# Seven block products in place of eight in the feed-forward networks of a two-block transformer kernel

## The chip, the cores and the metric

The kernel runs on one core of one Trainium2 chip. The metric is the device time of one execution in microseconds (us). Engines are named as in the profile: PE (TensorE, matmuls; PEld is its weight load), DVE (VectorE), ACT (ScalarE), POOL (GpSimd), SP (SyncE, which here issues the loads).

## What is computed

256 rows of 1024 float32 values pass through a first block (attention and mLSTM mixers, then a feed-forward network) and twice through a second block (network, mixer with attention over a memory, network). That makes five feed-forward networks, all of one size, 1024 to 2 x 2816 and back:

```
def swiglu(h, w_gate, w_up, w_down):
    return (jax.nn.silu(h @ w_gate) * (h @ w_up)) @ w_down

def second_block(...):
    for i in range(DEPTH_2):
        h = rmsnorm(x, ffn1_norm[i])
        x = x + 0.5 * swiglu(h, ffn1_w_gate[i], ffn1_w_up[i], ffn1_w_down[i])
        ...
        x = x + jnp.concatenate([o_s, o_m], axis=-1) @ w_out[i]
        h = rmsnorm(x, ffn2_norm[i])
        x = x + 0.5 * swiglu(h, ffn2_w_gate[i], ffn2_w_up[i], ffn2_w_down[i])
    return x
```

## The kernel before

**Tiles.** The rows are two tiles of 128, t = 0 and 1. The activations stand transposed in SBUF: u[t] is 8 tiles of 128 (of K = 1024) by 128 rows. The weights lie in DRAM as 228 pieces of 128 x 2048 float32 (1 MB): a piece is 512 of K by 512 columns (gate-up), or 256 of K by 1024 columns (down). SP loads them in the order of use into RAW_BUFS = 3 slots (`load_to`, L199).

**A float32 product in three matmuls.** Each operand is split into a high part, rounded to fp32r by a copy on ACT, and the rest, by a subtraction on DVE (`split`, L204 and L205: `wh`, `wl` for weights, `uh`/`ul` and `hh`/`hl` for activations). `mm3` then issues three matmuls of 512 columns: high by high, low by high, high by low. A piece is split in two halves of 128 x 1024, each in two parts of 512 columns (SPLIT_W); W_BUFS = 8 such halves of `wh` and of `wl` stand in SBUF, and `split_to` runs SPLIT_AHEAD = 4 halves ahead of the matmuls. A half's slot is free again when both row tiles have used it.

**A feed-forward network** (`ffn_body`) goes over NJ = 11 blocks of 256 hidden columns. For block j and tile t, `gu(t, j)` forms a bank of 256 gate and 256 up columns (8 x 3 = 24 matmuls); the gate is x(1 + tanh(x/2))/2 by a Tanh on ACT (L355), DVE's L356, and DVE's L358, which multiplies in the up half and gives `hid`. `turn` flips `hid` with the identity on PE (L154, four flips of 128 x 128 for both tiles) and splits it into `hh` and `hl`. `dn(t, j)` multiplies it into two banks that stay open over the whole network (12 matmuls). The order on PE is written out by hand: gu(0, j), dn(0, j-1), gu(1, j), dn(1, j-1), 72 matmuls and 4 flips a round; `fin(t)` (L402) adds the result to the residual. All the other engines' orders are the scheduler's, with elementwise work marked as urgent by `crit`.

**Between networks** stand the mixers: projections by the same `lin`, attention, norms (`row_rstd`, with POOL's powers at L261), and the projection `w_out` (L1197 adds it to the residual h).

## Time and profile before

| | |
|---|---|
| time, median of 3 runs | 1405.89 us (1405.14 to 1406.78) |
| time of the profiled execution | 1406.4 us, of which its span 1404.6 us |
| PE busy | 1385.3 us, 99% of the span, 6598 matmuls |
| DVE busy | 922.8 us, 66% |
| ACT busy | 763.6 us, 54% |
| POOL busy | 58.2 us, 4% |
| weight loads | 243.09 MB in SP's queue |

The profiled execution is 0.5 us above the median. A share of busy time is a mean over the networks, where all rounds are alike, and the mixers, where engines wait for one another; the stretches are read one by one below.

### The profile page before, as it was taken

To read this page: it belongs to the slowest core of one execution; us is meant where nothing else is said; L and a number is where in the kernel's file an instruction comes from. 1 tells how busy PE (TensorE), PEld (TensorE's weight loads), DVE (VectorE), ACT (ScalarE), POOL (GpSimd) and SP (SyncE) were. 2 spreads that over 40 slices of the span, in tenths; PEclk is the share of its full clock that TensorE was granted. 3 is DMA by queue.
4 is the path that set the end of the run, shared out by engine and by line. 5 is a ranking of instruction groups with operands and counts; after the bars stand their busy time and mean duration, and the time that the engine had idled before them with its cause. 6 is when DMAs were issued, how large, how long until landed. Compare 5 with 4: busy or idle time off the path is not lost.

```text
span 1404.6 us, 18011 instructions
## 1 busy us (share of the span) xinstructions
PE 1385.3 (99%) x6598; PEld 1126.6 (80%) x6598; DVE 922.8 (66%) x1789; ACT 763.6 (54%) x1527; POOL 58.2 (4%) x59
## 2 busy tenths in 40 slices
PE   8999999999999999999999999999999989999998
PEld 6777888888888888877888888888888767888887
DVE  7866587555585575768576665765756787755554
ACT  6556555444474454668565444644545568544442
POOL 0000000000010000022000000000000121000000
PEclk9999999999999999999999999999999999999999
DMA  8534546555446455454255555555454532455540
GB/s 291 174 122 158 180 142 237 192 191 189 180 157 233 180 180 180 168 197 161 91 183 191 195 187 194 207 191 197 164 206 155 182 120 94 172 188 194 192 180 30
DMA packets 37081, 246.59 MB, mean 176 GB/s; under 512 B 4736, under 2 KB 5760, under 8 KB 8064
## 3 DMA queue, kind: packets, MB, share of 16 engines
q1 hardware_dynamic: 35568, 243.09, 48.2%
q10 hardware_dynamic: 1424, 2.34, 0.5%
q8 instruction: 52, 0.85, 0.2%
q14 instruction: 37, 0.30, 0.1%
HBM read 244.37 MB, written 1.05 MB: 175 GB/s over the span
## 4 chain that ended last, share of the span: by engine, by line
PE 90%; DVE 6%; POOL 2%; ACT 1%; issue 1%; DMA 0%; SPq 0%; DVEq 0%; POOLq 0%; ACTq 0%
PE bank L149 86%; PE trbank L154 4%; POOL fac L261 2%; DVE wl L205 2%; DVE ms L953 1%; ACT p L454 1%; DVE nm L452 1%; DVE z L957 1%; DMA h<-in_x_dram 0%; DVE p L464 0%; DVE p L450 0%; DVE z L1015 0%; DVE p L1052 0%; DVE z L1017 0%; DVE z L1018 0%
## 5 line engine op out<-in xcount | busy, mean ns | idle before, releaser
L205 DVE TENSOR_TENSOR wl<-raw,wh 128x512 fp32r<-128x512 f32 x908 | 580.5, 686 | 194.4 <-ACT wh L204 187.6
L204 ACT CAST wh<-raw 128x512 fp32r<-128x512 f32 x908 | 513.0, 619 | 238.2 <-PE bank L149 227.9
L149 PE MATMUL bank<-wh,uh 128*128 128x512 f32 x1248 | 501.3, 402 | 0.0
L149 PE MATMUL bank<-wl,uh 128*128 128x512 f32 x1248 | 489.5, 392 | 0.0
L149 PE MATMUL bank<-wh,ul 128*128 128x512 f32 x1248 | 489.3, 392 | 0.0
L149 PEld LDWEIGHTS bank<-wh,ul 128*128 128x128 f32 x1248 | 234.6, 188 | 52.6
L149 PEld LDWEIGHTS bank<-wh,uh 128*128 128x128 f32 x1248 | 234.9, 188 | 48.8 <-issue 1.9
L149 PEld LDWEIGHTS bank<-wl,uh 128*128 128x128 f32 x1248 | 235.2, 188 | 46.1 <-DVE wl L205 0.3
L149 PE MATMUL bank<-wh,hh 128*128 128x512 f32 x440 | 172.8, 393 | 0.0
L149 PE MATMUL bank<-wl,hh 128*128 128x512 f32 x440 | 172.0, 391 | 0.0
L149 PE MATMUL bank<-wh,hl 128*128 128x512 f32 x440 | 172.0, 391 | 0.0
L355 ACT ACTIVATE th<-bank,rs 128x256 f32<-128x256 f32 x110 | 52.3, 475 | 179.2 <-PE bank L149 178.4
L356 DVE SCALAR_TENSOR_TENSOR th<-th,bank 128x256 f32<-128x256 f32 x110 | 46.3, 421 | 153.2 <-ACT th L355 153.2
L149 PEld LDWEIGHTS bank<-wl,hh 128*128 128x128 f32 x440 | 82.7, 188 | 18.0
L149 PEld LDWEIGHTS bank<-wh,hl 128*128 128x128 f32 x440 | 82.6, 188 | 17.9
L149 PEld LDWEIGHTS bank<-wh,hh 128*128 128x128 f32 x440 | 82.7, 188 | 17.6
L204 ACT CAST hh<-trbank 128x512 fp32r<-128x512 f32 (+1 forms) x60 | 33.1, 551 | 55.8 <-PE trbank L154 55.8
L261 POOL TENSOR_TENSOR r<-ms,mhalf 128x1 f32<-128x1 f32 x22 | 18.4, 838 | 909.5 <-DVE ms L271 909.5
L358 DVE SCALAR_TENSOR_TENSOR hid<-bank,rs,th 128x256 f32<-128x256 f32 x110 | 53.2, 484 | 3.6
L205 DVE TENSOR_TENSOR hl<-trbank,hh 128x512 fp32r<-128x512 f32 (+1 forms) x60 | 38.8, 646 | 16.5 <-ACT hh L204 13.5
L261 POOL TENSOR_TENSOR fac<-ms,mhalf 128x4 f32<-128x4 f32 (+2 forms) x26 | 38.4, 1477 | 246.8 <-DVE ms L954 139.3
L154 PEld LDWEIGHTS trbank<-cst,hid 128*128 128x128 f32 x220 | 27.6, 140 | 8.1
(223 smaller groups left out, 940.1 us busy)
## 6 DMA issues: line engine op xcount, KB each, us to landing
raw<-in_weights_dram SPq DMA_DIRECT2D x226, 1024.0 KB, 4.9
mem<-in_mem_dram ACTq DMA_DIRECT2D x4, 512.0 KB, 5.5
Tb<-in_rel_dram SPq DMA_DIRECT2D x3, 512.0 KB, 5.8
h<-in_x_dram SPq DMA_DIRECT2D x4, 256.0 KB, 3.8
raw<-in_weights_dram SPq DMA_DIRECT2D x2, 512.0 KB, 7.4
gf<-in_rows_dram SPq DMA_DIRECT2D x1, 512.0 KB, 4.1
out_dram<-h SPq DMA_DIRECT2D x2, 256.0 KB, 2.0
out_dram<-h SPq DMA_DIRECT2D x4, 128.0 KB, 1.8
```

The lines of the kernel that those rows point to most:

```text
L149: pe.matmul(out=out, lhsT=lhsT, rhs=rhs, start=start, stop=stop)
L154: pe.transpose(out=out, in_=in_, identity=ident if identity is None else identity)
L204: act.copy(out=hi, in_=src)
L205: dve.tensor_tensor(out=lo, in0=src, in1=hi.bitcast(F32), op=ALU.subtract)
L261: pool.tensor_tensor(out=dst, in0=src, in1=mhalf[:, 0:n], op=ALU.pow)
L355: act.activation(out=th, in_=acc[:, 0:256], func=AF.Tanh, scale=rh[t])
L356: dve.scalar_tensor_tensor(out=th, in0=th, scalar=1.0, in1=acc[:, 0:256], op0=ALU.add, op1=ALU.mult)
L358: dve.scalar_tensor_tensor(out=hd, in0=acc[:, 256:512], scalar=r2[t], in1=th, op0=ALU.mult, op1=ALU.mult)
L452: dve.tensor_reduce(out=nm, in_=s, axis=AX.X, op=ALU.max, negate=True)
L454: act.activation(out=p[:, j, a, 0:n], in_=s[:, j], func=AF.Exp, bias=nm[:, j:j + 1], accum_out=sums[:, j, a:a + 1])
L953: dve.tensor_reduce(out=ms, in_=sq, axis=AX.X, op=ALU.add)
L957: dve.tensor_tensor(out=v, in0=v, in1=fac.unsqueeze(2).to_broadcast([128, n, w]), op=ALU.mult)
```

## The change

In each network the first 5 blocks stay as they were (order gu(0), gu(1), dn(0), dn(1)). The other six form GROUPS = 3 groups of two blocks. The gate-up product of two blocks is a 2 x 2 by 2 x 2 block product: the row tiles and the halves of K on one side, the halves of K and the two blocks on the other. It is formed from seven block products P1 to P7 instead of eight (Strassen's scheme in Winograd's form), each 12 matmuls. For this

- four sums of activation blocks are formed and split once a network (`group_operands`, after the first block);
- four sums of weight pieces are formed in each group: two by DVE (L267, `raw<-raw,rawx` and `tn<-raw,rawx`, 128 x 1024 twice each), two by accumulating DMAs that POOL issues (L277: `rawx<-rawx`, for P7, and `tn<-raw`, for P4). `rawx` are two slots for the pieces b12 and b22, `tn` is one slot for a sum;
- the bank results are joined by seven DVE adds of 128 x 512 (L562, `jo`) and a copy on ACT (L576, c11).

The gate is one Silu on ACT; L356 of before has no counterpart. Splits are 1024 wide (SPLIT_W), ACT's copies of weights keep their written order (`in_order`), W_BUFS is 6, and `w_out` goes over columns first. The memory tile has one buffer for two. The load order of a group is b11, dn_a, b12, b22, b21, dn_b. ACT loads its tables 8 times for 3.

```diff
+P_FFN = 3 * NJ
 
 RAW_BUFS = 3
-W_BUFS = 8
+W_BUFS = 6
 C_BUFS = 11
 C2_BUFS = 10
 SPLIT_AHEAD = 4
 LOAD_AHEAD = 2
 CRIT = 300
-SPLIT_W = 512
+SPLIT_W = 1024
+
+GROUPS = 3
...
     def load_to(n):
         while stream["load"] < min(n, NP):
             i = stream["load"]
-            r = wp.tile([128, 2048], F32, tag="raw", bufs=RAW_BUFS, name="raw")
+            if i in kept:
+                r = kept[i][0].tile([128, 2048], F32, tag="tx", bufs=2, name="rawx")
+            else:
+                r = wp.tile([128, 2048], F32, tag="raw", bufs=RAW_BUFS, name="raw")
             n_dma = 2 if i == 0 else 1
             for q in range(n_dma):
                 w = 2048 // n_dma
-                nc.sync.dma_start(out=r[:, w * q:w * q + w], in_=weights[i, :, w * q:w * q + w])
+                nc.sync.dma_start(out=r[:, w * q:w * q + w], in_=weights[piece_at.get(i, i), :, w * q:w * q + w])
             raws[i] = r
             stream["load"] += 1
...
     def split(hi, lo, src):
-        act.copy(out=hi, in_=src)
+        c = act.copy(out=hi, in_=src)
         dve.tensor_tensor(out=lo, in0=src, in1=hi.bitcast(F32), op=ALU.subtract)
+        return c
+
+    order = [None]
+
+    def in_order(inst):
+
+        if order[0] is not None:
+            tc.add_manual_dep(inst.ins, order[0].ins.name,
+                              mybir.DependencyInfo(mybir.DependencyClass.NoSync, mybir.DependencyReason.DATA),
+                              reason="order of the operands")
+        order[0] = inst
 
     def split_to(n):
 
-        while stream["split"] < min(n, 2 * NP):
-            i, m = divmod(stream["split"], 2)
-            load_to(i + 1 + LOAD_AHEAD)
-            r = raws[i]
+        while stream["split"] < min(n, len(jobs)):
+            key, piece, work = jobs[stream["split"]]
+            load_to(piece + 1 + LOAD_AHEAD)
+            r = work()
             hi = wp.tile([128, 1024], FR, tag="wh", bufs=W_BUFS, name="wh")
             lo = wp.tile([128, 1024], FR, tag="wl", bufs=W_BUFS, name="wl")
             for s in range(0, 1024, SPLIT_W):
-                split(hi[:, s:s + SPLIT_W], lo[:, s:s + SPLIT_W], r[:, 1024 * m + s:1024 * m + s + SPLIT_W])
-            parts[i, m] = (hi, lo)
+                in_order(split(hi[:, s:s + SPLIT_W], lo[:, s:s + SPLIT_W], r[:, s:s + SPLIT_W]))
+            parts[key] = (hi, lo)
             stream["split"] += 1
...
+    def group_jobs(i, pool_, dn):
+
+
+        b11, b12, b22, b21 = i, i + 2, i + 3, i + 4
+        kept[b12] = kept[b22] = pool_
+        s = lambda m: slice(1024 * m, 1024 * m + 1024)
+        total = []
+
+        def job(name, piece, work):
+            for m in range(2):
+                add_job(((i, name), m), piece, lambda m=m: work(m))
+
+        def add(out, a, b):
+            dve.tensor_tensor(out=out, in0=a, in1=b, op=ALU.add)
+
+        def t2(m):
+            if m == 0:
+                total.append(pool_[0].tile([128, 2048], F32, tag="tn", bufs=1, name="tn"))
+            add(raws[b11][:, s(m)], raws[b11][:, s(m)], raws[b12][:, s(m)])
+            add(total[0][:, s(m)], raws[b11][:, s(m)], raws[b22][:, s(m)])
+            return total[0][:, s(m)]
+
+        def dma_add(out, a):
+            pool.dma_start(out=out, in_=a, accum_op=ALU.add)
+
+        def b21_(m):
+            if m == 0:
+                dma_add(raws[b12], raws[b22])
+            return raws[b21][:, s(m)]
+
+        def b11_(m):
+            if m == 0:
+                dma_add(total[0], raws[b21])
+            return raws[b11][:, s(m)]
+
+        def t3(m):
+            return raws[b12][:, s(m)]
+
+        def t4(m):
+            return total[0][:, s(m)]
+
+        job("P1", b11, lambda m: raws[b11][:, s(m)])
+        plain(dn[0])
+        job("P6", b22, t2)
+        job("P2", b21, b21_)
+        job("P5", b21, b11_)
+        plain(dn[1])
+        job("P3", b21, lambda m: raws[b22][:, s(m)])
+        job("P7", b21, t3)
+        job("P4", b21, t4)
...
+        nc_ = NJ - 2 * GROUPS
...
+        for j in range(nc_):
+            take(("gu", j), 2)
+            if 1 <= j < nc_ - 1:
+                take(("dn", j - 1))
...
+        for g in range(GROUPS):
+            j = nc_ + 2 * g
+            a, b = (j - 2, j - 1) if g == 0 else (j - 1, j - 2)
+            plan["group", g] = i
+            plan["dn", a], plan["dn", b] = i + 1, i + 5
+            g0, g1 = source(("gu", j)), source(("gu", j + 1))
+            piece_at.update(enumerate((g0, source(("dn", a)), g1, g1 + 1, g0 + 1, source(("dn", b))), i))
+            group_jobs(i, plan["pool"], (i + 1, i + 5))
+            i += 6
+        for j in ((NJ - 2, NJ - 1) if GROUPS else ()):
...
-            acc = lin(u[t], gup(j))
-            ev = Ready()
-            if j == 0:
-                with crit():
-                    rh[t], r2[t] = scaled(r[t], 0.5), scaled(r[t], r[t], 0.5)
-
+        hidT, hid_ready, hids = {}, {}, {}
+        n_conv = NJ - 2 * GROUPS
+
+        def element(t, j, acc):
+
+            hid_ready[t, j] = Ready()
             with crit():
                 th = fp.tile([128, 256], F32, tag="th", name="th")
-                act.activation(out=th, in_=acc[:, 0:256], func=AF.Tanh, scale=rh[t])
-                dve.scalar_tensor_tensor(out=th, in0=th, scalar=1.0, in1=acc[:, 0:256], op0=ALU.add, op1=ALU.mult)
-                hd = fp.tile([128, 256], F32, tag="hid", bufs=4, name="hid")
-                dve.scalar_tensor_tensor(out=hd, in0=acc[:, 256:512], scalar=r2[t], in1=th, op0=ALU.mult, op1=ALU.mult)
-            hids[t] = hd
-            hid_ready[t, j] = ev
-            if j == NJ - 1:
-                side.spawn(turn((t,), j))
-            elif t == 1:
-                side.spawn(turn((0, 1), j))
+                act.activation(out=th, in_=acc[:, 0:256], func=AF.Silu, scale=r[t])
+                hd = fp.tile([128, 256], F32, tag="hid", bufs=5, name="hid")
+                dve.scalar_tensor_tensor(out=hd, in0=acc[:, 256:512], scalar=r[t], in1=th, op0=ALU.mult, op1=ALU.mult)
+            hids[t, j] = hd
+
+        def gu(t, j):
+            i = plan["gu", j]
+            acc = lin(u[t], (i, i + 1))
+            element(t, j, acc)
+            if t == 1:
+                side.spawn(turn((0, 1), j, 3.46))
             side.run()
...
+            hh = fp.tile([128, 2 * n, 128], FR, tag=f"hh{n}{ts[0]}", bufs=n, name="hh")
+            hl = fp.tile([128, 2 * n, 128], FR, tag=f"hl{n}{ts[0]}", bufs=n, name="hl")
...
+        def group_operands():
+            x11, x12, x21, x22 = (full.pop((id(u[t][2]), k)) for t in range(2) for k in (0, 4))
+            sh = fp.tile([128, 4, 4, 128], FR, tag="sh", bufs=1, name="sh")
+            sl = fp.tile([128, 4, 4, 128], FR, tag="sl", bufs=1, name="sl")
+
+            dve.tensor_tensor(out=x22, in0=x21, in1=x22, op=ALU.subtract)
+            dve.tensor_tensor(out=x21, in0=x11, in1=x21, op=ALU.subtract)
+            dve.tensor_tensor(out=x11, in0=x22, in1=x11, op=ALU.subtract)
+            dve.tensor_tensor(out=x12, in0=x12, in1=x11, op=ALU.add)
+            for n, (name, x) in enumerate((("P6", x11), ("P5", x22), ("P7", x21), ("P3", x12))):
+                split(sh[:, n], sl[:, n], x)
+                S[name] = sh[:, n], sl[:, n]
+            for name, t, k in (("P1", 0, 0), ("P2", 0, 4), ("P4", 1, 4)):
+                S[name] = u[t][0][:, k:k + 4], u[t][1][:, k:k + 4]
+
+        def group(g):
+
+            j = n_conv + 2 * g
+            a, b = (j - 2, j - 1) if g == 0 else (j - 1, j - 2)
+            last = g == GROUPS - 1
+            i = plan["group", g]
+
+            def joined(x, y, op, into=None):
+                o = fp.tile([128, 512], F32, tag="jo", bufs=4, name="jo") if into is None else into
+                with crit():
+                    dve.tensor_tensor(out=o, in0=x, in1=y, op=op)
+                return o
+
+            def prod(name):
+                acc = bank()
+                xh, xl = S[name]
+                for k in range(4):
+                    wh, wl = half((i, name), k // 2, 512)
+                    mm3(acc, xh[:, k], xl[:, k], wh[:, k % 2], wl[:, k % 2], k == 0, k == 3)
+                return acc
+
+            c11 = fp.tile([128, 512], F32, tag="jo", bufs=4, name="jo")
+            p1_ = prod("P1")
+            with crit():
+                act.copy(out=c11, in_=p1_)
+            dn(1, a)
+            dn(0, a)
+            U = joined(prod("P6"), c11, ALU.add)
+            joined(prod("P2"), c11, ALU.add, c11)
+            element(0, j, c11)
+            if last:
+                side.spawn(turn((0,), j, 4.2))
+            V = joined(prod("P5"), U, ALU.subtract)
+            dn(0, b)
+            c12 = joined(prod("P3"), V, ALU.add)
+            element(0, j + 1, c12)
+            if last:
+                side.spawn(turn((0,), j + 1, 4.2))
+            dn(1, b)
+            p7 = prod("P7")
+            joined(V, p7, ALU.subtract, V)
+            element(1, j + 1, V)
+            joined(p7, U, ALU.add, U)
+            side.spawn(turn((1,) if last else (0, 1), j + 1, 4.9))
+            joined(prod("P4"), U, ALU.add, U)
+            element(1, j, U)
+            side.spawn(turn((1,) if last else (0, 1), j, 4.2))
...
+        for j in range(n_conv):
+            more = 1 <= j < n_conv - 1
             gu(0, j)
-            if j:
+            gu(1, j)
+            if more:
                 dn(0, j - 1)
-            gu(1, j)
-            if j:
                 dn(1, j - 1)
-            if during and j == 5:
+            if j == 0:
+                group_operands()
+            if during and j == n_conv - 1:
                 during()
-        j = NJ - 1
-        gu(0, j)
-        dn(0, j - 1)
-        gu(1, j)
-        dn(1, j - 1, (0,))
+        for g in range(GROUPS):
+            group(g)
+        j = NJ - 2
         dn(0, j)
+        dn(1, j + 1, (0,))
+        dn(0, j + 1, by_c=True)
         fin(0)
-        dn(1, j - 1, (1,))
-        dn(1, j)
+        dn(1, j + 1, (1,))
+        dn(1, j, by_c=True)
         fin(1)
...
-            for t in range(2):
-                for c in range(2):
+            for c in range(2):
+                for t in range(2):
...
-            ms = mp.tile([128, 1024], F32, tag="mem", bufs=2, name="mem")
+            ms = mp.tile([128, 1024], F32, tag="mem", bufs=1, name="mem")
```

The names in the order of instructions: `raw` is a loaded piece, `rawx` one of the two pieces b12 and b22, `tn` the sum of pieces, `jo` a joined result. On DVE, the steady rounds of a network before stand like this (`th` and `hid` once for each row tile, splits between them):

```order
L205 TENSOR_TENSOR wl<-raw,wh 128x512 x6
L356 SCALAR_TENSOR_TENSOR th<-th,bank 128x256
L358 SCALAR_TENSOR_TENSOR hid<-bank,rs,th 128x256
L205 TENSOR_TENSOR wl<-raw,wh 128x512 x6
L205 TENSOR_TENSOR hl<-trbank,hh 128x512
L356 SCALAR_TENSOR_TENSOR th<-th,bank 128x256
L358 SCALAR_TENSOR_TENSOR hid<-bank,rs,th 128x256
```

Of the change, DVE's rows in the third network from the end of the second group (its P7 and P4) to the third group's P6:

```order
L475 SCALAR_TENSOR_TENSOR hid<-jo,r,th 128x256
L223 TENSOR_TENSOR wl<-raw,wh 128x1024
L562 TENSOR_TENSOR jo<-bank,jo 128x512
L223 TENSOR_TENSOR wl<-raw,wh 128x1024
L475 SCALAR_TENSOR_TENSOR hid<-jo,r,th 128x256
L267 TENSOR_TENSOR raw<-raw,rawx 128x1024
L223 TENSOR_TENSOR hl<-trbank,hh 128x512 x2
L267 TENSOR_TENSOR tn<-raw,rawx 128x1024
L267 TENSOR_TENSOR raw<-raw,rawx 128x1024
L223 TENSOR_TENSOR wl<-tn,wh 128x1024
L267 TENSOR_TENSOR tn<-raw,rawx 128x1024
L223 TENSOR_TENSOR wl<-tn,wh 128x1024
```

The `jo` is the one that needs P4, the last product of the group; the four sums stand behind it, with both splits of `hl` between them, and the second half of P6's operand (the last row) behind them all. On SP, the loads of the groups of that network, with the numbers of the tiles:

```order
L217 DMA raw_6837<-in_weights_dram 128x2048
L217 DMA raw_6906<-in_weights_dram 128x2048
L217 DMA raw_7074<-in_weights_dram 128x2048
L217 DMA rawx_7016<-in_weights_dram 128x2048
L217 DMA rawx_7045<-in_weights_dram 128x2048
L217 DMA raw_7076<-in_weights_dram 128x2048
L217 DMA raw_7122<-in_weights_dram 128x2048
L217 DMA raw_7182<-in_weights_dram 128x2048
```

raw_6837, raw_6906, raw_7074, rawx_7016, rawx_7045 and raw_7076 are b11, dn_a, b21, b12, b22 and dn_b of the second group; raw_7122 is b11 of the third and takes the slot of raw_7074, which the second accumulating DMA (`tn<-raw`) reads. On POOL, the accumulating DMAs of that network, with the numbers of the tiles:

```order
L277 DMA rawx_6728<-rawx_6750 128x2048
L277 DMA tn_6811<-raw_6807 128x2048
L277 DMA rawx_7016<-rawx_7045 128x2048
L277 DMA tn_7078<-raw_7074 128x2048
L277 DMA rawx_7292<-rawx_7321 128x2048
L277 DMA tn_7354<-raw_7350 128x2048
```

None of these stood in the program before; the two of a group are issued back to back in one queue.

## Rows read from the trace of the kernel before

**Rows 1.** The page: span, and the chain that ended last by engine.

```profile
span 1404.6 us, 18011 instructions
...
PE 90%; DVE 6%; POOL 2%; ACT 1%; issue 1%; DMA 0%; SPq 0%; DVEq 0%; POOLq 0%; ACTq 0%
```

**Rows 2.** The chain in the third network: start us, us, what.

```profile
757.68 0.44 PE trbank L154 x4
758.12 16.46 PE bank L149 x72
...
884.91 8.24 PE bank L149 x36
893.15 0.22 PE trbank L154 x2
893.37 1.39 PE bank L149 x6
```

**Rows 3.** Busy time of each engine in one round and in two mixers.

```profile
core 0: us, PE busy (x) PEld busy (x) DVE busy (x) ACT busy (x) POOL busy (x), PEclk, DMA share, GB/s
...
758.12:775.02 16.90, 16.90 (x77) 13.91 (x77) 9.93 (x18) 8.18 (x15) 0.00 (x0) 1.00 0.52 189
588.30:713.50 125.20, 122.17 (x691) 97.95 (x689) 89.88 (x197) 85.93 (x208) 18.32 (x16) 1.00 0.42 150
1084.40:1217.10 132.70, 125.60 (x672) 99.53 (x671) 99.87 (x215) 87.10 (x213) 22.25 (x17) 0.99 0.37 130
```

**Rows 4.** DVE's timeline in that round: start, us, instruction, [idle before].

```profile
762.80 0.42 DVE L356 SCALAR_TENSOR_TENSOR th<-th,bank 128x256 f32<-128x256 f32 x1 [3.34 <-ACT th L355]
763.26 0.48 DVE L358 SCALAR_TENSOR_TENSOR hid<-bank,rs,th 128x256 f32<-128x256 f32 x1
767.10 4.00 DVE L205 TENSOR_TENSOR wl<-raw,wh 128x512 fp32r<-128x512 f32 x6 [3.35 <-ACT wh L204]
...
771.89 3.69 DVE L205 TENSOR_TENSOR wl<-raw,wh 128x512 fp32r<-128x512 f32 x6
```

**Rows 5.** DVE's timeline where one network ends: a 1024-wide product.

```profile
397.85 0.41 DVE L205 TENSOR_TENSOR hl<-trbank,hh 128x256 fp32r<-128x256 f32 x1
...
399.81 1.22 DVE L1269 TENSOR_TENSOR h<-h,gf 128x1024 f32<-128x1024 f32 x1
400.94 0.69 DVE L205 TENSOR_TENSOR ul<-uf,uh 128x512 fp32r<-128x512 f32 x1
```

**Rows 6.** ACT's timeline there: a 1024-wide activation.

```profile
397.31 0.37 ACT L204 CAST hh<-trbank 128x256 fp32r<-128x256 f32 x1 [1.84 <-PE trbank L154]
...
404.26 1.04 ACT L267 ACTIVATE junk<-h 128x1024 f32<-128x1024 f32 x1
405.21 0.19 ACT L267 ACTIVATION_READ_ACCUMULATOR junk<-h 128x1 f32 x1
```

**Rows 7.** Groups by line: count, busy us and mean ns, idle before.

```profile
L205 DVE TENSOR_TENSOR wl<-raw,wh 128x512 fp32r<-128x512 f32 x908 | 580.5, 686 | 194.4 <-ACT wh L204 187.6
L355 ACT ACTIVATE th<-bank,rs 128x256 f32<-128x256 f32 x110 | 52.3, 475 | 179.2 <-PE bank L149 178.4 <-DVE hl L205 0.7
L356 DVE SCALAR_TENSOR_TENSOR th<-th,bank 128x256 f32<-128x256 f32 x110 | 46.3, 421 | 153.2 <-ACT th L355 153.2
L1197 DVE TENSOR_TENSOR h<-bank,h 128x512 f32<-128x512 f32 x8 | 5.5, 688 | 11.2 <-PE bank L149 11.2
L933 ACT ACT_TABLE_LOAD x1 | 1.3, 1283 | 0.0
```

**Rows 8.** What SP's queue waited for: us in total, times, longest.

```profile
SPq L199 <- DVE wl L205: 1211.2, 213, 19.3
```

**Rows 9.** The page: the loads' queue, and the time from issue to landing.

```profile
q1 hardware_dynamic: 35568, 243.09, 48.2%
...
raw<-in_weights_dram SPq DMA_DIRECT2D x226, 1024.0 KB, 4.9
```

More of the change, by code (lines that the diff above doesn't have):

```diff
@@ L188, with add_job, plain @@
     stream = {"load": 0, "split": 0}
-    raws, parts = {}, {}
+    raws, parts, kept = {}, {}, {}
     NP = weights.shape[0]
+    jobs, at_job = [], {}
+    piece_at = {}
+    def add_job(key, piece, work):
+        at_job[key] = len(jobs)
+        jobs.append((key, piece, work))
+    def plain(i):
+        for m in range(2):
+            add_job((i, m), i, lambda i=i, m=m: raws[i][:, 1024 * m:1024 * m + 1024])
     def load_to(n):
@@ L287, in new_u @@
         return uh, ul, []
+    full = {}
     def put_T(u, k0, n, src, gains=None, gain1=None, keep=None):
@@ L297, in put_T @@
         if gains is not None:
-            s = tmp.tile([128, 4, 128], F32, tag="uf", name="uf") if keep is None else keep[:, k0:k0 + n]
+            s = tmp.tile([128, 4, 128], F32, tag="uf", bufs=4, name="uf") if keep is None else keep[:, k0:k0 + n]
+            full[id(u[2]), k0] = s
             dve.tensor_tensor(out=s, in0=b3, op=ALU.mult,
@@ L333, in ffn, with ffn_plan, source, take @@
             ffn_body(fp, *args)
+    def ffn_plan(p0):
+        plan = {"pool": [None]}
+        i = p0
+        def source(key):
+            kind, j = key
+            if kind == "dn":
+                return p0 + (3 * j + 4 if j < NJ - 1 else 32)
+            return p0 if j == 0 else p0 + 3 * j - 1
+        nc_ = NJ - 2 * GROUPS
+        def take(key, n=1):
+            nonlocal i
+            plan[key] = i
+            for q in range(n):
+                piece_at[i + q] = source(key) + q
+            i += n
+        for j in range(nc_):
+            take(("gu", j), 2)
+            if 1 <= j < nc_ - 1:
+                take(("dn", j - 1))
+        for j in range(nc_):
+            for q in range(2):
+                plain(plan["gu", j] + q)
+            if 1 <= j < nc_ - 1:
+                plain(plan["dn", j - 1])
+        for g in range(GROUPS):
[8 more added lines that the diff above has]
+        for j in ((NJ - 2, NJ - 1) if GROUPS else ()):
+            take(("dn", j))
+            plain(plan["dn", j])
+        assert i == p0 + P_FFN
+        return plan
@@ L376, in turn @@
             b = trbank()
-            for a, hd in enumerate(mine):
+            for a, t in enumerate(ts):
+                hd = hids.pop((t, j))
                 for i in range(2):
@@ L384, in turn, with dn @@
                 side.ready(hid_ready[t, j], 3.36)
-        def dn(t, j, kts=(0, 1)):
+        started = set()
+        def dn(t, j, kts=(0, 1), by_c=False):
             if accd[t] is None:
@@ L390, in dn @@
             hh, hl = hidT[t, j]
-            order = [(c, k) for c in range(2) for k in kts] if j == NJ - 1 else [(c, k) for k in kts for c in range(2)]
-            for c, k in order:
-                wh, wl = half(dnp(j), k, 512)
-                mm3(accd[t][c], hh[:, k], hl[:, k], wh[:, c], wl[:, c], j == 0 and k == 0, j == NJ - 1 and k == 1)
+            done[t] += len(kts)
+            order = [(c, k) for c in range(2) for k in kts] if by_c else [(c, k) for k in kts for c in range(2)]
+            for n, (c, k) in enumerate(order):
+                wh, wl = half(plan["dn", j], k, 512)
+                first = (t, c) not in started
+                started.add((t, c))
+                mm3(accd[t][c], hh[:, k], hl[:, k], wh[:, c], wl[:, c], first,
+                    done[t] == 2 * NJ and (c, k) == [o for o in order if o[0] == c][-1])
+        done = [0, 0]
         def fin(t):
@@ L407, in fin @@
                 finish(t)
-        for j in range(NJ - 1):
+        S = {}
+        def group_operands():
[11 more added lines that the diff above has]
+                S[name] = u[t][0][:, k:k + 4], u[t][1][:, k:k + 4]
@@ L1191, in second_mix @@
         res = [[], []]
-        for t in range(2):
-            for c in range(2):
+        for c in range(2):
+            for t in range(2):
                 acc = lin((get_oT(t)[0], get_oT(t)[1], o_ready[t]), (p1 + 2 * c, p1 + 2 * c + 1))
@@ L1245, in memory_kv, with plan_ffn @@
             side.spawn(task())
-    P_FFN = 3 * NJ
+    plans = {}
+    for n in range(30):
+        plain(n)
+    p = 30
+    def plan_ffn():
+        nonlocal p
+        plans[p] = ffn_plan(p)
+        p += P_FFN
+    plan_ffn()
+    for layer in range(2):
+        plan_ffn()
+        for n in range(16):
+            plain(p + n)
+        p += 16
+        plan_ffn()
+    assert p == NP
     p = 0
```

30 lines of the change are left out of this document (12 added, 18 removed).

## The prediction

> **What bounds the kernel now.** First the page: its chain that ended last is PE for 90%, DVE for 6% [rows 1]. So matmuls that go away are worth their time wherever PE is the engine that is waited for. Then the chain in one network: 72 matmuls in 16.46 us, four flips in 0.44, and the next round at once [rows 2]. That is 16.46 / 72 = 0.2286 us a matmul of 512 columns (8.24 / 36 gives 0.2289; I take 0.2288) and 0.11 a flip; a round takes 16.90 us, with no gap. Then the same round by engines: PE busy for all of its 16.90, DVE for 9.93, ACT for 8.18 [rows 3], so that DVE has 7 us to spare in each; its timeline shows them as two waits of 3.3 us, one for the gate, one for ACT's casts [rows 4]. The mixers are another matter: there DVE is busy for 89.88 of 125.20 and 99.87 of 132.70 us, and PE for 3 and 7 us less than the stretch [rows 3]. SP's loads wait nearly all the time for DVE to release a slot of `raw` [rows 8]: the queue is never behind now.
>
> **What is removed.** A group of two blocks had 8 x 12 = 96 gate-up matmuls and has 84. Three groups in five networks: 15 x 12 = 180 matmuls, 180 x 0.2288 = 41.2 us, 8.24 a network. PE alone would end at 1406.4 - 41.2 = 1365.2. DVE loses L356, 110 x 421 ns = 46.3 us [rows 7], in stretches where it had slack.
>
> **What DVE gets in a group.** Prices are distances between starts. A 512-wide split: (3.69 - 0.69) / 5 = 0.60 us [rows 4]; a 1024-wide product of two operands: from 399.81 to 400.94, 1.13 us [rows 5]. In a group stand 18 weight splits of 1024 (14 for the seven products, 4 for two down pieces): 18 x 1.13 = 20.3. Four sums of 1024: 4 x 1.13 = 4.5. Seven joins, which read a bank as L1197 does (688 ns, as long as a split [rows 7]): 7 x 0.60 = 4.2. Four `hid` at about 0.42 from start to start (0.48 long [rows 4]): 1.7. Two `hl` at 0.60: 1.2. Together 31.9 us. PE's part of a group is 84 + 48 matmuls and 8 flips: 132 x 0.2288 + 0.88 = 31.1 us; two rounds of before are 33.8. So DVE goes from 2 x 9.93 = 19.9 us busy in 33.8 to a little more than PE has. ACT has 18 copies at 0.95 (the distance of starts of a 1024-wide one [rows 6]), four gates at 0.475 [rows 7], a 512-wide copy and two `hh`: some 21 us, and doesn't bound. If DVE only has to keep up on average, a group loses 0.8 us of its 2.75; the loss is more where PE needs something that stands late in DVE's order.
>
> **Walk through the order.** I laid a network's last stretch out by hand, in the order printed above, with these prices, from the first P1 to the last matmul.
> - *Into the first group.* The conventional rounds leave DVE slack, so the buffers are full: only the first sums are late, 0.4 us.
> - *From group to group.* After P4, PE has P1 (12 matmuls), eight flips, and two down products (24): 36 x 0.2288 + 0.88 = 9.1 us until the next P6, 10.5 until P6's second half. DVE has behind P4: a join, a split of 1.13 (ACT's gate of 0.475 runs beside it), `hid`, four sums, two `hl`, a split, ACT's cast of the last sum (0.95 and a handover), and the split itself: 0.6 + 1.1 + 0.4 + 4.5 + 1.2 + 1.1 + 1.0 + 1.1 = 11.0. It is late by 0.5 us at a boundary that DVE reaches on time. In the walk it is 0.65 at the first, where a lead from the conventional rounds is still there, and 1.7 at the second, where DVE arrives late, since it needs 31.9 us for a group that PE does in 31.1 and the six weight buffers let it run no further ahead. Within the last group 0.5 more.
> - *The end of a network.* The flips of the row tile t = 1 for the last two blocks share one buffer of `hh`: the second split waits until dn(1, 10) has read the first, and then 0.37 for `hh` on ACT [rows 6], 0.41 for `hl` on DVE [rows 5], and on ACT first the 1.04 of `junk`, which `fin(0)` starts [rows 6]. With the wait for P4's join, gate and `hid`, 2.8 us. Before, the last rounds' chain shows flips and matmuls without a gap [rows 2].
>
> Sum of the losses: 0.4 + 0.65 + 1.7 + 0.5 + 2.8 = 6.05 us of 8.24; net 2.2 a network, 11 in all: 41.2 - 5 x 6.05 = 10.95.
>
> **The accumulating DMAs.** Nothing like them is in the trace. A load of 1 MB keeps the 16 engines for 0.482 x 1404.6 / 243.09 = 2.8 us, and lands 4.9 us after issue [rows 1, 9]. Below, an accumulation is one such pass, 2.8 us; above, three (two reads and a write one after another), 8.4. The second of a group reads b21's slot, into which b11 of the next group is loaded; SP's queue is in order, and five more loads stand behind it. By the walk, the two have 10.5 us from their issue before the load is late for the third group's P1 (one place a network; ahead of the first groups there is slack). Two at 2.8 are 5.6, two at 4.2 are 8.4: nothing is late. Two at 5.6 are 11.2, late by some 1 us a network, 5 in all. Two at 8.4 are 16.8, late by 6 us a network, 31 in all. I take a price up to 4.2, nearer to the load's row, and so nothing.
>
> On this the Trainium skill speaks against the change: in "Collectives: The Full Stack", on why ReduceScatter is half of AllGather, it says that a reducing transfer reads two sources and runs at about half the rate of a copy. No row here shows an accumulation; by that rule it is 5.6 us, and the sum would be 5 us more, 1400.
>
> **What goes at nothing.** `group_operands` (four sums at 0.60, four splits at 0.60 on DVE: 4.8 us) stands behind the first block, where each conventional round leaves 7 us of DVE [rows 3]; were that cover gone, 4.8 a network. The down products' new order in the conventional rounds has the same matmuls; six halves of weights are just one round's, and the next round's splits have the second gate-up product and both down products to come in, so 0. Five more table loads on ACT at 1.283 us [rows 7] stand at the edges of networks and beside the mixers' exponentials; bounds 0 and 6.4, and I take 0, since most lie behind PE work. In the mixers a half is split in 1.13 instead of 2 x 0.60: some 124 halves, 8.7 us less DVE work, where DVE is the busy one [rows 3]; against it, splits twice as long stand ahead of urgent work, and there are two buffers fewer. I take 0, within 3 either way.
>
> **Sum.** Against the profiled execution: 1406.4 - 41.2 + 30.2 = 1395.4; it stands 0.5 above the median of the runs, so 1395 us.
>
> **The rivals.**
> - *PE stays the bound.* The scheduler's rows are the order, but their times are my walk's: if the buffers carry a longer lead into the groups, or the starts lie closer than 1.13, DVE needs less than PE. Then each loss shrinks to the end of the network: 1365 with none, 1365.2 + 5 x 2.8 = 1379 with that one. For it: DVE has 7 us of slack in every conventional round [rows 3]. Against it: six buffers hold no more than a round.
> - *The transfers bound: slower.* If an accumulation is more than some 5.3 us, b11 of the third group lands late, and behind it in SP's queue all other loads of that group, on which PE waits. At three passes 1395 + 31 = 1426. The point from which it decides: above 11 us for a network the gain is gone, that is when the two together need 10.5 + 2.2 = 12.7 us, 6.4 each. For it: the loads take 52% of the engines in a round already [rows 3], and these come on top, from one queue. Against it: the half of the engines that is free. Beside it the Trainium skill, "SBUF — State Buffer", warns that DVE's two-port operations starve GpSimd of the port with which it writes descriptors; the operations on DVE in a group are tensor_tensor, of which the page says that they have no such mode. No run here shows either.
> - *DVE takes all of it.* If a start costs 1.22, as the 1024-wide row is long [rows 5], instead of 1.13, 22 operations in a group make 2.0 us more: 33.9 a group, as long as two rounds of before. The first group still has the lead; two periods then lose 2.8 each, and the end of the network 2.8: 8.4 of the 8.24 saved, 1407, no change.
>
> **How the numbers follow.** My forecast, from 1388 to 1403 by the walk's bounds: 0.41. PE as the bound, 1365 to 1380: 0.17. Transfers, 1409 to 1426: 0.32 (with it the mixers' and the tables' losses). No change: 0.10. A measurement of this kernel can tell 0.2%, 2.8 us, from no change. Faster 0.58, the same 0.10, slower 0.32. The range goes from 1370, which leaves half of the PE-bound case's low end out, to 1424.
>
> **What would show it.** In the changed profile: 6418 matmuls and flips on PE's 6598 - 180 (and fewer or more by the records missing); DVE over 80% busy, and in a group near 100%, with a mean near 1.2 us for the 1024-wide splits; a group period of 31.7 to 32.8 us between P1s; in the chain DVE's splits of `tn` ahead of P6, and `hh`/`hl` at each network's end, 2 to 3 us; the DMAs of L277 landing within 10 us of issue, and SP's loads waiting for DVE and not for them. It would be wrong if L277 lands later than 10 us, if the chain in the groups is PE alone, or if the stretches of the mixers differ by over 3 us.

## The result and the profile after

The changed kernel takes 1421.71 us (1420.88 to 1424.69), the kernel before 1405.78 beside it: ratio 1.0117, interval 1.0099 to 1.0134. It is slower by 15.9 us, where 1395 was forecast. PE has the 180 matmuls less; the page shows what became of their 41.2 us (its head with busy times, the chain by engine, the queues, and the DMA issues with KB and us to landing):

```profile
span 1420.0 us, 17210 instructions
...
PE 1369.3 (96%) x6418; PEld 1093.1 (77%) x6418; DVE 1102.1 (78%) x1505; ACT 833.9 (59%) x1208; POOL 82.9 (6%) x89
...
q1 hardware_dynamic: 35568, 243.09, 47.2%
q0 software_dynamic: 4320, 31.46, 11.0%
...
PE 73%; DVE 18%; ACT 4%; issue 3%; POOL 1%; DMA 1%; DVEq 0%; POOLq 0%; ACTq 0%
...
rawx<-rawx POOLq DMA_DIRECT2D x15, 1024.0 KB, 7.0
tn<-raw POOLq DMA_DIRECT2D x15, 1024.0 KB, 7.7
```

PE's share of the chain falls from 90% to 73% and DVE's rises from 6% to 18% [rows 1]. To see where, I cut both spans at the first flips of `hid` and at the start of the last addition to the residual (`fin`) of each network. First the changed kernel, then the one before: from the first network to the second, the mixer behind the second with its lead into the third, the third network, and the last mixer (columns as in [rows 3]).

```profile
402.62:422.16 19.54, 18.02 (x75) 14.55 (x75) 16.80 (x30) 15.40 (x24) 2.56 (x3) 0.91 0.65 250
597.76:737.84 140.08, 134.83 (x724) 106.71 (x723) 98.91 (x176) 92.50 (x185) 19.43 (x16) 0.98 0.46 167
737.84:909.47 171.63, 167.04 (x745) 134.23 (x743) 138.36 (x154) 98.68 (x119) 5.79 (x7) 1.00 0.66 211
1100.87:1247.65 146.78, 137.37 (x706) 107.50 (x705) 108.95 (x194) 94.16 (x190) 20.77 (x17) 0.98 0.42 149
```

```profile
403.23:418.17 14.94, 14.94 (x72) 12.29 (x71) 14.45 (x35) 13.03 (x24) 3.16 (x3) 1.00 0.49 166
592.01:726.46 134.45, 131.42 (x726) 105.35 (x725) 98.31 (x212) 90.99 (x216) 17.95 (x16) 1.00 0.45 161
726.46:898.45 171.99, 171.99 (x780) 141.65 (x779) 102.97 (x178) 85.09 (x158) 0.93 (x1) 1.00 0.50 183
1088.09:1230.01 141.92, 134.82 (x708) 106.91 (x707) 108.28 (x230) 92.20 (x221) 21.88 (x17) 0.99 0.41 142
```

Three stretches outside the networks lose 4.6, 5.6 and 4.9 us, 15.1 of the 15.9. The third network, with 36 matmuls less, is as long as before, and so are the five networks together, cut in this way (865.0 us for 865.5). They are not alike: the second and the fourth are 1.8 us longer each, the others 1.3, 0.4 and 2.3 shorter. Only the second and the fourth also prepare the memory for the mixer that follows (`memory_prep`), and the change moved this work from behind the sixth block to behind the fifth, just ahead of the groups, which neither the list of the change nor the prediction names. The granted clock says something more: 0.91, 0.98 and 0.98 in the three stretches outside, where it was 1.00, 1.00 and 0.99.

Within the third network the chain from its second to its third group reads like this (start us, us, what):

```profile
855.83 6.42 PE bank L152 x28
...
863.37 0.53 DVE hl L223
863.90 0.08 issue
863.98 0.68 DVE hl L223
864.66 1.13 DVE tn L267
865.80 1.13 DVE raw L267
866.93 1.21 DVE wl L223
868.14 1.15 DVE tn L267
869.29 0.02 issue
869.31 1.06 ACT wh L222
870.37 0.02 issue
870.39 1.24 DVE wl L223
871.67 4.20 PE bank L152 x17
```

That is the order printed ahead of the prediction, row by row: two `hl`, sums, the first half's split, the last sum, ACT's cast of it, the last split, and then PE goes on with P6.

### The profile page after: what moved, and what is told of

It reads as the page before. It is cut to its first block, busy times and chain, and to the rows that moved or that the text cites. A ratio compares the mean times of both kernels' runs of the same rounds, so it can differ in the third digit from the quotient of the medians.

```text
span 1420.0 us, 17210 instructions
## 1 busy us (share of the span) xinstructions
PE 1369.3 (96%) x6418; PEld 1093.1 (77%) x6418; DVE 1102.1 (78%) x1505; ACT 833.9 (59%) x1208; POOL 82.9 (6%) x89
## 3 DMA queue, kind: packets, MB, share of 16 engines
q1 hardware_dynamic: 35568, 243.09, 47.2%
q10 hardware_dynamic: 1424, 2.34, 0.5%
## 4 chain that ended last, share of the span: by engine, by line
PE 73%; DVE 18%; ACT 4%; issue 3%; POOL 1%; DMA 1%; DVEq 0%; POOLq 0%; ACTq 0%
PE bank L152 70%; DVE wl L223 8%; PE trbank L157 4%; ACT wh L222 2%; DVE tn L267 2%; POOL fac L341 1%; DVE jo L562 1%; DVE raw L267 1%; DVE hl L223 1%; DVE nm L645 1%; DMA mem<-in_mem_dram 1%; DVE hid L475 1%; DVE ms L1147 0%; ACT hh L222 0%; ACT p L647 0%
## 5 line engine op out<-in xcount | busy, mean ns | idle before, releaser
L223 DVE TENSOR_TENSOR wl<-raw,wh 128x1024 fp32r<-128x1024 f32 x424 | 512.9, 1221 | 132.1 <-ACT wh L222 123.3
L222 ACT CAST wh<-raw 128x1024 fp32r<-128x1024 f32 x424 | 439.0, 1050 | 176.9 <-PE bank L152 159.8
L152 PE MATMUL bank<-wh,uh 128*128 128x512 f32 x948 | 380.7, 402 | 2.2 <-ACT uh L222 2.0
L152 PE MATMUL bank<-wh,ul 128*128 128x512 f32 x948 | 374.5, 395 | 0.2 <-DVE ul L223 0.2
L152 PE MATMUL bank<-wl,uh 128*128 128x512 f32 x948 | 373.2, 394 | 0.0
L152 PEld LDWEIGHTS bank<-wh,hh 128*128 128x128 f32 x440 | 82.7, 188 | 26.1 <-ACT hh L222 10.5
L152 PE MATMUL bank<-wl,sh 128*128 128x512 f32 x240 | 95.3, 397 | 6.8 <-DVE wl L223 6.8
L152 PE MATMUL bank<-wh,sh 128*128 128x512 f32 x240 | 95.2, 397 | 0.0
L152 PE MATMUL bank<-wh,sl 128*128 128x512 f32 x240 | 94.1, 392 | 0.0
L223 DVE TENSOR_TENSOR wl<-tn,wh 128x1024 fp32r<-128x1024 f32 x60 | 72.9, 1222 | 18.2 <-ACT wh L222 17.4
L223 DVE TENSOR_TENSOR wl<-rawx,wh 128x1024 fp32r<-128x1024 f32 x60 | 70.6, 1218 | 0.8 <-ACT wh L222 0.8
L562 DVE TENSOR_TENSOR jo<-bank,jo 128x512 f32<-128x512 f32 x90 | 61.7, 686 | 2.1 <-PE bank L152 2.0
```

What stands on the lines that cost most here:

```text
L152: pe.matmul(out=out, lhsT=lhsT, rhs=rhs, start=start, stop=stop)
L222: c = act.copy(out=hi, in_=src)
L223: dve.tensor_tensor(out=lo, in0=src, in1=hi.bitcast(F32), op=ALU.subtract)
L562: dve.tensor_tensor(out=o, in0=x, in1=y, op=op)
```

## The experiments

Times are medians beside runs of the kernel before on the same chip; the ratio to it stands with its interval.

| run | us | ratio (interval) |
|---|---|---|
| changed kernel | 1421.71 | 1.0117 (1.0099 to 1.0134) |
| g0 | 1429.70 | 1.0176 (1.0150 to 1.0203) |
| a_mix512 | 1413.52 | 1.0056 (1.0041 to 1.0071) |
| b_wout | 1406.95 | 1.0010 (1.0000 to 1.0019) |
| b_split1024 | 1412.31 | 1.0044 (1.0028 to 1.0061) |
| b_silu | 1409.03 | 1.0021 (1.0012 to 1.0031) |
| b_w6 | 1414.06 | 1.0058 (1.0043 to 1.0073) |
| a_dveadd | 1467.44 | 1.0448 (1.0428 to 1.0467) |
| a_narrow | 1411.09 | 1.0039 (1.0025 to 1.0052) |
| a_tail | 1406.40 | 1.0003 (0.9994 to 1.0013) |
| a_tail_exp | 1401.81 | 0.9972 (0.9963 to 0.9981) |
| a_noorder | 1401.80 | 0.9974 (0.9963 to 0.9984) |
| a_dma3 | 1442.23 | 1.0259 (1.0241 to 1.0277) |
| a_m8 | 1398.85 | 0.9947 (0.9930 to 0.9963) |
| a_m8_old | 1403.29 | 0.9986 (0.9976 to 0.9996) |
| a_g2 | 1400.15 | 0.9957 (0.9942 to 0.9973) |
| a_m8_g2 | 1396.50 | 0.9938 (0.9923 to 0.9953) |
| a_m8_g1 | 1402.01 | 0.9975 (0.9965 to 0.9985) |

### Groups or the rest: g0

```diff
-GROUPS = 3
+GROUPS = 0
```

> The changed kernel with no groups: all 11 blocks conventional, the other edits (1024-wide splits, six weight buffers, casts in written order, w_out over columns first, Silu gate) kept. Theory 1, that the edits outside the groups cost the 14 us by which the stretches between the networks grew (4.9, 4.1, 5.2 us and less): 1417 to 1421 us, with the growth in the same stretches. Rival, that work left over from the groups is what makes the stretches behind the networks late: 1404 to 1408, and those stretches as before.

1429.70, above both. The groups, then, are worth some 8.0 us (1429.70 - 1421.71; the two intervals leave some 4 either way), and all the other edits together cost some 24. The two mixers stay long without any group (139.9 and 149.4 us between the same marks), so for them the rival, a backlog left by the groups, falls. Between the first two networks it does not: that stretch is 16.2 us without groups, 19.5 with them and 14.9 before. One thing is not like the kernel before: the order at a network's end is the one made for groups, so a part of the 24 us, at most the 5.6 by which its five networks are longer, belongs to that.

### Which of the rest: b_split1024, a_mix512, a_narrow

```diff
# b_split1024: the kernel before
-SPLIT_W = 512
+SPLIT_W = 1024
# a_mix512, a_narrow: the changed kernel
-            for s in range(0, 1024, SPLIT_W):
+            w = 512 if key[0] in narrow else SPLIT_W
+            for s in range(0, 1024, w):
...
# narrow: the mixers' pieces; in a_narrow the networks' plain pieces too
```

> The kernel before, with all splits 1024 wide. If the width is what delays urgent work in the mixers: 1412 to 1416, with stalls of PE at the norms and a granted clock under 1.0 there, the networks' rounds at 16.9 us. If shorter DVE time (8.7 us less in the mixers) pays for it: 1403 to 1407.

> The changed kernel, with the weight splits of the mixers (not of the networks) back at 512 columns. If it is the width of the splits in the mixers that delays urgent work there: 8 to 10 us less than the changed kernel, 1411 to 1414, and the granted clock in the mixers back near 1.0. If it is the order of w_out, the buffers or the networks' own pieces: within 2 us of 1421.7.

> The changed kernel with splits 512 wide everywhere but in the groups (mixers, conventional blocks, last down pieces). If wide splits of the networks' first and last pieces are what delays the norms at the networks' ends: 2 to 4 us less than with narrow splits in the mixers alone (1413.5), most of it between the first and the second network (18.5 us, 14.9 before). If the groups' backlog delays them: 1413.

Wide splits alone cost the kernel before 6.7 us (1412.31 against 1405.64), at a granted clock of 1.000 over the span of the profiled execution; taken out of the changed kernel's mixers they give 8.2 back, and out of the networks' ends and beginnings 2.4 more, at the edge of what can be told. The chain in the first of the later mixers of the changed kernel shows one such place:

```profile
617.37 1.65 POOL fac L341
...
619.65 0.78 DVE wl L223
620.43 0.36 issue
620.79 3.49 DVE wl L223 x3
624.27 0.61 DVE ms L1147
...
625.22 1.65 POOL fac L341
```

The next norm (`ms`, then POOL's power, on which the next step waits) stands behind three splits of 1.13 us and more. There is less DVE work in the mixers than with halves in two parts, but what is urgent can only slip in between two splits, and the pieces are now twice as long. This way of the loss is read from the rows, not shown by them alone: before, too, a norm of that mixer stood behind splits, five narrow ones in 3.09 us (from 615.29). That the width costs is shown by the runs. Between the first two networks ACT's order holds PE up; ACT's rows and then PE's:

```profile
401.48 1.05 ACT L222 CAST wh<-raw 128x1024 fp32r<-128x1024 f32 x1 [2.37 <-PE bank L152]
402.44 1.05 ACT L347 ACTIVATE junk<-h 128x1024 f32<-128x1024 f32 x1
403.39 0.19 ACT L347 ACTIVATION_READ_ACCUMULATOR junk<-h 128x1 f32 x1
403.48 0.60 ACT L222 CAST uh<-uf 128x512 fp32r<-128x512 f32 x1
```

```profile
404.14 0.50 PE L152 MATMUL bank<-wh,uh 128*128 128x512 f32 x1 [1.99 <-ACT uh L222]
```

PE waits 1.99 us for `uh`, which stands behind a wide cast and a sum of squares. But the width is not what makes this stretch long: with wide splits alone it is 14.95 us (b_split1024), as before, and with narrow ones it is 17.9 in a_mix512 and in a_narrow alike, so the gain that was expected there for a_narrow did not come. Six buffers with the order of `w_out` make it 16.1 (b_w6), g0 has 16.2; the rest came with the groups, and no run has taken it back (17.8 in the best version below).

### The order of w_out and the buffers: b_wout, b_w6

```diff
# b_wout
-            for t in range(2):
-                for c in range(2):
+            for c in range(2):
+                for t in range(2):
...
# b_w6: that, and
-W_BUFS = 8
+W_BUFS = 6
```

> The kernel before, with w_out alone going over columns first. If that order costs, since the first row tile's norm starts after three quarters of w_out instead of half: 1 to 2 us at each of three networks, 1409 to 1412. If the flips and splits of the first tile are hidden either way: 1406.

> The kernel before with w_out over columns first and six weight buffers for eight. If the missing buffers cost lead in the mixers: 3 to 8 us over the run with that order alone (1406.95), in the mixers. And in the networks, whose order here still runs two down products between the gate-up products, a stall a round is possible: each 1 us a round would be 50 us. If they cost nothing: 1407.

The order costs 1.3 us, at the edge of what can be told; six buffers 7.1 more, in the mixers and at the networks' edges; no round of a network has a stall. In the second of the later mixers PE now waits for a cast of weights just ahead of w_out, which it didn't before:

```profile
1193.73 0.63 PE L154 MATMUL trbank<-cst,o 128*128 128x128 f32 x4 [1.75 <-ACT wh L204]
```

### The gate's tables: b_silu

```diff
-                act.activation(out=th, in_=acc[:, 0:256], func=AF.Tanh, scale=rh[t])
-                dve.scalar_tensor_tensor(out=th, in0=th, scalar=1.0, in1=acc[:, 0:256], op0=ALU.add, op1=ALU.mult)
+                act.activation(out=th, in_=acc[:, 0:256], func=AF.Silu, scale=r[t])
...
```

> The kernel before with the Silu gate alone: one multiply less on DVE for each gate, and ACT's table loads that come with it. If a table load stands in a mixer's chain (in the changed kernel ACT loads one at 627.95 and one at 1137.81, where PE waited 1.3 to 1.8 us more than before): 2 to 5 us slower, 1408 to 1411, in the two mixers and nowhere else. If the loads are hidden: 1405 to 1406.

3.65 us slower, with less work on DVE. In the last mixer PE's wait for `p` grows from 2.18 to 4.04 us, behind a table load (ACT's timeline, then PE's):

```profile
1126.20 1.28 ACT L449 ACT_TABLE_LOAD   x1
```

```profile
1132.19 0.64 PE L154 MATMUL trbank<-cst,p 128*128 128x128 f32 x2 [4.04 <-DVE p L1047]
```

Other waits shrink by as much: over the whole execution PE waits 15.5 us, for 15.7 before. What grew is the time at a lower granted clock: 0.996 over the span for 0.999, and (0.999 - 0.996) x 1408.2 = 4.2 us is about the whole difference. So the tables' price seems to be paid in the clock, after waits that moved (last section); this run does not separate the two.

### The accumulating DMAs: a_dveadd, a_dma3

```diff
# a_dveadd: both sums on DVE
+            add(total[0][:, s(m)], total[0][:, s(m)], raws[b21][:, s(m)])
...
+            add(raws[b12][:, s(m)], raws[b12][:, s(m)], raws[b22][:, s(m)])
# a_dma3 (on a_tail_exp, below): a third sum by DMA
-            add(raws[b11][:, s(m)], raws[b11][:, s(m)], raws[b12][:, s(m)])
+            if m == 0:
+                dma_add(raws[b11], raws[b12])
```

> The changed kernel with the two accumulating DMAs of a group done by DVE, four more 1024-wide sums of 1.13 us in a group. If DVE bounds the groups: 4.5 us a group for all that is not slack, 45 to 68 us slower than the changed kernel, 1465 to 1490. If the DMAs are what is late in the groups: no slower than 1422.

> The same as the run with the early table, with a third of a group's four sums (b11 + b12) by an accumulating DMA. DVE has 2.3 us less in a group, 29.6 for PE's 31.1. If DVE's whole work bounds the groups: 1 to 2 us less a network, 5 to 10 in all. If it is the order at the group's boundary, the sum must land (7 us) before P6's operand: late by 1 us and more a boundary, 0 to 10 us slower.

Four more DVE sums a group cost 45.7 us, 3.0 a group for 4.5 us of work. In the third network nothing of it falls into the stretch up to the head of the second group (29.2 us in both kernels), and 5.0 into the next (37.9 us for 32.9). From the first boundary on, then, DVE is the bound, and the two DMAs save far more than they cost. A third sum by DMA is 40.4 us slower than its base: of DVE's waits

```profile
DVE tn L269 <- DMA raw<-rawx: 53.6, 15, 4.4
```

(us in total, times, longest): it lands 7.7 us after its issue, too late for P6. In both runs a part of the loss goes through the granted clock (last section): 0.983 over the span for 0.994, up to 16 us, and 0.979 for 0.998, up to 27. A sum pays as a DMA where its operand is needed late (P7, P4), not at the head of a group.

### The end of a network and the early table: a_tail, a_tail_exp, a_noorder

```diff
# a_tail: a_narrow, and the last flips of t = 1 use the two wide buffers, t = 0 has two of its own
-            hh = fp.tile([128, 2 * n, 128], FR, tag=f"hh{n}{ts[0]}", bufs=n, name="hh")
+            wide = n == 2 or ts[0] == 1
+            hh = fp.tile([128, 4 if wide else 2, 128], FR, tag=f"hh{wide}", bufs=2, name="hh")
...
# a_tail_exp: that, and behind the last gate ahead of a mixer
+            act.activation(out=small(1, "pre"), in_=th[:, 0:1], func=AF.Exp, scale=0.0)
# a_noorder: that, and in_order only for the groups' casts
```

> The changed kernel with narrow splits outside the groups (1411.1) and, at a network's end, two buffers of hh and hl for each row tile's last two blocks instead of one. If the shared buffer makes the end of a network late (0.47, 0.56 and 0.87 us of PE waiting there in the changed kernel): 1 to 2.5 us a network, 1399 to 1406. If it is the join, gate and hid behind the last product: 1409 to 1411.

> The same, and an exponential of one column right after the last gate of the two networks ahead of a mixer, so that ACT loads the mixer's table there. If the table loads in the mixers' chains cost: 2 to 4 us less than the run without it, and the waits for qkT and p in the mixers as before the change. If they are hidden: no difference.

> The same as the run with the early table, with ACT's casts bound to their written order in the groups alone. If the written order holds back urgent work in the mixers: 1 to 4 us less. If the six buffers set that order anyway: no difference beyond 1.5 us.

Two buffers give 4.7 us, 0.9 a network; this is what the chain at the third network's end showed in the changed kernel, PE waiting for a pair of `hh` and `hl` that could not start earlier:

```profile
890.51 5.96 PE bank L152 x26
896.48 0.02 issue
896.50 0.38 ACT hh L222
896.88 0.02 issue
896.91 0.42 DVE hl L223
```

The early table gives 4.6 more, and the kernel is now faster than the one before. PE's wait for `p` in the last mixer and its waits for `qkT` fall as expected, from 3.8 to 2.0 us and from 2.5 to 0.7 (2.2 and 0.7 before the change). But all of PE's waits together fall only from 37.5 to 36.7, while the granted clock, in the median of the ten runs of each, rises from 0.996 to 0.999, which is 4.2 us of 1402. The order of casts makes no difference.

### Buffers and order again, and how many groups: a_m8, a_m8_old, a_g2, a_m8_g2, a_m8_g1

```diff
# a_m8: a_tail_exp, and every fourth half of a later mixer's pieces, up to w_out, from its own pool
+                hi = xw[0].tile([128, 1024], FR, tag="whx", bufs=2, name="wh")
+                lo = xw[0].tile([128, 1024], FR, tag="wlx", bufs=2, name="wl")
...
# a_m8_old: that in all mixers, w_out over row tiles first
# a_g2, a_m8_g2: GROUPS = 2; a_m8_g1: GROUPS = 1
```

> The run with the early table (1401.8), with two more weight halves in the two later mixers, from space that is free there, up to w_out. If six buffers cost in the mixers: 2 to 4 us less, the second of these mixers back from 147 toward 143 us. If not: within 1.5 us.

> The same in all three mixers, and w_out in them in the order of before (row tiles first), which needs eight halves. If buffers and order cost 7.1 and 1.3 us as in the single runs, of which a part lies in the networks: 4 to 8 us less than the run with the early table, 1394 to 1398. If the order is hidden: as the run with eight halves alone.

> The run with the early table (1401.8), with two groups a network instead of three. By the walk the first boundary costs 0.65 us and the second 1.7, against 2.75 saved in each group: the third group gains about 1 us a network, so 5 us slower, 1405 to 1408. If DVE takes all that a third group saves: 1400 to 1403. If a group saves nearly all of its 2.75: 1412 and more.

> The best run so far (1398.85, three groups, eight halves in the mixers) with two groups a network. If the boundary terms found so far are right (the third group pays nothing): 1397 to 1399. If the eight halves change that: 1402 and more.

> The same with one group a network: no boundary between groups at all. If a boundary takes a group's 2.75 us nearly whole, one group is as good as two or three: 1397 to 1401. If the first boundary costs 0.65, as in the walk, the second group gains some 2 us a network: 1406 to 1410.

Eight halves in the mixers give 3.0 us (the last mixer 144.1 instead of 147.0). The run with the old order of `w_out`, in which the first mixer also gets the extra halves, was expected to give more and loses 4.4: its last mixer is 1.4 us shorter, but the stretch to the first network's flips 4.4 longer. Which of its two edits does that I have not found out; 1.8 of it is a wait of PE for `uh` (at 221.4) that the run before it does not have.

With one, two and three groups the mended kernel takes 1402.01, 1396.50 and 1398.85 us. The second group gains 5.5 us, 1.1 a network. The third gains nothing: it loses 2.35, at the edge of what can be told, and without the extra halves, too, two groups are no slower than three (1400.15 against 1401.81). In the traces with three and with two groups four of the five networks are 0.1 to 0.2 us longer with the third group, and the second, which prepares the memory, 1.8. Two groups with all the mendings is the best version found: 0.9938 of the kernel before.

```profile
span 1396.1 us, 17788 instructions
...
PE 1365.4 (98%) x6478; PEld 1101.6 (79%) x6478; DVE 1044.7 (75%) x1754; ACT 831.0 (60%) x1509; POOL 82.9 (6%) x79
...
PE 78%; DVE 15%; ACT 3%; issue 2%; POOL 2%; DMA 0%; SPq 0%; DVEq 0%; POOLq 0%; ACTq 0%
```

## Why the prediction was wrong

**The step that failed** is the one on "what goes at nothing". It took the mixers as "0, within 3 either way" and the table loads as "0, since most lie behind PE work"; the order of `w_out` it did not name. The two later mixers came out 5.6 and 4.9 us longer, beyond the 3 that the prediction gave as a sign of being wrong. Put alone into the kernel before, wide splits cost 6.7 us, six buffers 7.1, the order of w_out 1.3 and the Silu's tables 3.65: 18.8 together. For the splits I had reckoned DVE's work, 8.7 us less, and set the delay of urgent work against it without a price. [Rows 3] had the warning: in the mixers DVE was busy for about three quarters of the time and PE still waited, so DVE's amount of work alone could not set the time there; how soon it gets to the next norm had to be priced as well.

**The walk through the groups** had the right chain, and boundaries that were too small. The prices held: 1.13 us from start to start. In the third network, from the flips ahead of the first group to those at the head of the second, and from there to the head of the third (columns as in [rows 3]):

```profile
800.03:829.18 29.15, 29.15 (x132) 24.01 (x131) 24.45 (x27) 17.40 (x20) 0.00 (x0) 1.00 0.68 230
829.18:862.07 32.89, 31.89 (x142) 25.44 (x140) 31.74 (x37) 21.17 (x25) 1.72 (x2) 1.00 0.79 253
```

In the first of these PE never waits, where the walk had 0.4. The second is 1.8 us longer than the 31.1 of PE's own work, where the walk had 0.65 for this boundary. By the runs, too, the second group gains 1.1 of its 2.75 a network, which leaves 1.65. The third gains nothing, so its boundary and the rest of it cost at least 2.75, where the walk had 1.7 and 0.5. The walk also took the five networks as alike; in the second and the fourth the period from head to head is 34.5 and 34.1 us, with the memory's work in it or just ahead of it. It gave the groups 11 us net; against g0 they bring 8.0, with some 4 either way. The end of a network was put at 2.8; two buffers took 0.9 of it away. The rest, behind P4's join, was not tried.

**The sum by runs**: 18.8 for the four edits less 8.0 for the groups is 10.8, and 15.9 was measured. The 5 us between them (24 us for g0 against 18.8) are no more than the runs' intervals leave open (some 3.7 us for g0 and 3.4 for the four sums together); they may also come from the edits together, or from the end of a network in g0. I could not split them.

**The rivals.** The time lies in the slower rival's 1409 to 1426, and through it in the range from 1370 to 1424, by luck: the reason given there is wrong, the DMAs were not late for PE. What did come stands in that chance only in brackets, "with it the mixers' and the tables' losses", without a price. The engines are busy for 0.110 x 1420.0 / 30 = 5.2 us with one accumulation, against 0.472 x 1420.0 / 243.09 = 2.76 us a MB, 2.9 for a load. That is above my 4.2, but two of them, 10.4, still fit the 10.5 us of the walk. SP did wait for them:

```profile
SPq L217 <- DMA tn<-raw: 233.3, 15, 19.5
```

But no wait of PE or DVE names a weight load, and ACT's come to 7.2 us in the whole execution (5.2 before), 0.6 of them in the third network: next to nothing was late. The rule from the Trainium skill, "Collectives: The Full Stack", why ReduceScatter is half of AllGather (two source reads, about half a copy's rate), agrees with 5.2 against 2.9. The price of 5.6 was near; the 5 us of delay drawn from it did not come. The rival on starvation of descriptors ("SBUF — State Buffer" of the Trainium skill, the "DVE blocks DMA" trap) is not borne out by any row: all 30 landed within 6.9 to 9.2 us. That DVE takes all that a group saves was given 0.10; the outcome is that of the third group alone, and its reason, a start in 1.22 us, did not hold (1.13). PE stayed the bound in the first group alone.

## What to carry to other kernels

An edit that only makes the same work coarser, or its buffers fewer, has its price where another stage waits for a short urgent operation: read the chain there, and reckon the longest thing that can stand in front, not the sum of work. When a bundle wins at its core, undo its side edits one at a time: here the core was worth some 8 us and its company cost some 24. And count a scheme's gain for each repetition: two groups paid, the third did not, since DVE needed as long for a group as PE; look, too, at what other work an edit pushes into so tight a stretch, here the memory's.

## What the hardware showed that I had not expected

PE's granted clock fell after some of the new waits, which costs time on top of the waits. In windows of 4 us of the changed kernel (the column before the last two is the granted clock):

```profile
404.00:408.00 4.00, 3.86 (x13) 2.79 (x14) 2.79 (x7) 3.63 (x6) 2.01 (x2) 0.72 1.01 426
632.00:636.00 4.00, 1.91 (x10) 1.46 (x12) 3.61 (x9) 2.95 (x5) 0.00 (x0) 0.81 0.00 0
636.00:640.00 4.00, 4.00 (x13) 2.76 (x10) 3.50 (x5) 0.11 (x1) 0.00 (x0) 0.50 0.79 262
1136.00:1140.00 4.00, 4.00 (x14) 3.19 (x13) 3.34 (x6) 3.97 (x9) 0.48 (x1) 0.57 0.13 20
1168.00:1172.00 4.00, 4.00 (x23) 2.71 (x22) 2.15 (x6) 0.00 (x0) 1.64 (x1) 0.70 0.68 215
```

0.50 is the lower of the two levels, 1.2 GHz for 2.4. PE had waited 1.99 us at 404.14, 0.81 and 1.32 at 632.78 and 634.92, 2.22 at 1135.79 and 3.20 at 1166.09; other waits (1.46 us at 660.32) were followed by no fall. Before, there was one such place, in the last mixer. Over the span the clock is 0.994 instead of 0.999: (1 - 0.994) x 1420.0 = 8.5 us of full-speed time against 1.4, so up to some 7 of the 15.9 us are matmuls at the lower level, inside the sums above (PE also waited in a part of that time). The mended version with two groups runs at 1.000. That these waits set off the falls was read from the rows, not tried by itself; the two runs on the tables come nearest, where time and clock moved together and the sum of PE's waits hardly did.
